# Two block products on half of the tokens ahead of a feed-forward stage, in place of a pair of feature tiles in token halves

## The chip, the cores and the metric

The kernel runs on one core of one Trainium2 chip. The metric is the device time of one execution in microseconds (us), lower is better. Of the kernel before, three runs are known: 2374.69 (median), 2373.43 and 2375.28 us.

## The reference

Two layers on 512 tokens of width 1024. In each layer a feed-forward stage stands before and another behind a mixing stage (three kinds of attention, whose results are gated and merged):

```python
def _swiglu(t, w_gate, w_up, w_down):
    return (jax.nn.silu(t @ w_gate) * (t @ w_up)) @ w_down

f = _swiglu(_rmsnorm(h, ffn1_pre_g[l]), ffn1_w_gate[l], ffn1_w_up[l], ffn1_w_down[l])
h = h + 0.5 * _rmsnorm(f, ffn1_post_g[l])
...                                     # mixing: h = h + rmsnorm(merged @ w_out)
f = _swiglu(_rmsnorm(h, ffn2_pre_g[l]), ffn2_w_gate[l], ffn2_w_up[l], ffn2_w_down[l])
h = h + 0.5 * _rmsnorm(f, ffn2_post_g[l])
```

The hidden width is 2816, that is 22 feature tiles of 128. All is float32. The change concerns the four feed-forward stages alone, called a0, c0 (layer 0) and a1, c1 (layer 1).

## The kernel before

**Numbers in two parts.** TensorE reads a float32 operand here as a high part (rounded to the type fp32r) and a low part (the rest). `split` (L185) makes them: ScalarE casts the high part (L188), VectorE subtracts it from the source to get the low (L189; L191 and L192 where a scale is applied). `mm3` (L212) makes a product of three matmuls: high by high (L214), and two of high by low (L215, L216). A unit of weights is 128 x 1024 numbers, 512 KB. It is fetched by a DMA of the queue SP (`fetch`, at most four in the ring called raw), and split into the rings wh and wl of four units each, or into other places named by `tags`.

**Two ways to multiply.** A *plain pair* is two feature tiles: `gates` (L824) computes the gate of both for all 512 tokens, 48 matmuls of 512 columns, and `ups` (L831) the up part; `hidden` (L659) multiplies Silu(gate) by up. *Block products* compute four feature tiles at once: tokens and model width are halved, gate and up are the two column blocks of the weights, and seven products of 256 tokens by 512 of width by 512 columns, 24 matmuls each, take the place of eight (`gate_up`, L730). Products 0 and 1 need only the activations of the first 256 tokens; 6 needs those of the second 256; 2 to 5 need sums of activation blocks (`sums`, L696: VectorE, with `whole`, L681, `block_sum`, L687, and the splits into the tiles ag). The weight sides of products 2, 3, 5 and 6 are differences as well: VectorE subtracts (L337, L340, L345, L349) before the split. Product 0's sum stays in two PSUM banks through products 3, 5 and 6. After each product the banks are copied by ScalarE (L751) or added by VectorE (L753) into tiles c, and L760 multiplies the two halves of a result. PSUM has eight banks, four called mm and four called z.

**The order of a stage** (`ffn`, L644). Feature tiles 16 and 17 (`EARLY`) are computed by `halved` (L797): half 0, with the tokens of tiles 0 and 1, may run while the token tiles 2 and 3 are still being normalized and transposed (`Sub.chain`, L623); half 1 follows when all are ready. Each half is 96 matmuls of 256 columns, high parts first. Its weights `ug` and `uu` are loaded in the stage before, which is told of them in `marks["early"]`. Then come the gates of pair 18 with Silu at once (`ahead`), the groups of block products for tiles 0 to 15 (`TG`, first group in the order `FIRST`, others in `ORDER`), and between the pieces the calls of `sums`. The down stage (`product`, L871, in the same seven products, on z banks) follows, with the ups of pair 18 and the pair 20 between its products.

**The queue.** `Queue` (L372) holds the jobs of TensorE in this order. When a job starts, its units are loaded, and after that four units of the following jobs (`load_ahead`, L413) unless `hold` is set; `weave` (L455) lets the chain of a token tile come in between at times counted in TensorE's work. The framework under it places semaphores and buffers, and settles the final order in each engine's queue with a model of its own; `in_order` (L166) and `keep_in_program_order` fix parts by hand.

**The kernel's start** (`begin`, L1639). Stage a0 has no stage before it. `begin` fetches the token tiles and first weights, spreads a gain row over the partitions into two mm banks by matmuls (`spread`, L550), computes the statistics, scales (L1676), transposes (L1667) and splits the first two tiles, all in one order for ScalarE and VectorE; the gains are copied to SBUF at L1706 behind the scaling of tile 2.

The early job as it stands:

```python
Q.add(ug + uu, lambda: halved(EARLY, ug, uu, 0), src.ready((0, 1)))
Q.add([], lambda: halved(EARLY, ug, uu, 1), src.ready(range(NT)))
...
add_sums()
Q.add(pairs[0][0], lambda: gates(18, pairs[0][0], True))
add_sums()
todo = turns(TG[0])
some(8)
```

Of the kernel before, what the change touches and what calls it, by code (L numbers as in the profile page):

```python
# [9 lines left out]
F32 = mybir.dt.float32  # L10
F32R = mybir.dt.float32r
BF16 = mybir.dt.bfloat16
AF = mybir.ActivationFunctionType
# [4 lines left out]
P = 128  # L18
# [4 lines left out]
def kernel(  # L23
# [620 lines left out]
    def ffn(l, src, wg, wu, wd, dst, name, spare, aside=None):  # L644
# [152 lines left out]
        def halved(f, ug, uu, half):  # L797
            if half == 0:
                st["p"] = [pbank("mm", f"p{x}{name}_{f + m}") for x in "gu" for m in range(2)]
            else:  # L800
                Q.hold, Q.pinned = False, True
                Q.load_ahead()
                Q.pinned = False
                next(summed)
            c = HALVES[half]

            for uns, pts in ((ug, st["p"][:2]), (uu, st["p"][2:])):
                for low in (False, True):
                    for un in uns:
                        for k, (m, pt) in itertools.product(range(un.nk), enumerate(pts)):  # L810
                            kk, cols = un.k0 + k, slice(m * P, (m + 1) * P)
                            wh, wl = un.h[:, k, cols], un.l[:, k, cols]
                            ah, al = act(kk, c)
                            if low:
                                nc.tensor.matmul(pt[:, c], wh, al, start=False, stop=False, skip_group_check=True)
                                nc.tensor.matmul(pt[:, c], wl, ah, start=False, stop=kk == ND - 1, skip_group_check=True)
                            else:
                                nc.tensor.matmul(pt[:, c], wh, ah, start=kk == 0, stop=False, skip_group_check=True)
                            yield (1 + low) * S // 2 * PE_US
            if half == 1:  # L820
                for m in range(2):
                    hidden(f + m, st["p"][m], st["p"][2 + m])
# [110 lines left out]
        marks["early"] = ug + uu  # L933
        for un, place in zip(ug + uu, ("tri", "tri", (spare, spare), (spare, spare))):
            un.tags = place
# [6 lines left out]
        pairs = [(wpair(wg[l], ND, f * P, f"g{name}_{f}"), wpair(wu[l], ND, f * P, f"u{name}_{f}")) for f in (18, 20)]  # L942
# [8 lines left out]
        for g in TG[1:]:  # L951
            todo = turns(g)
            some(2)
            over, later[:] = later[1:], later[:1]
            behind()
            some(7)
            later[:] = over
        todo = downs(0)
# [680 lines left out]
    def begin():  # L1639
# [9 lines left out]
        ug = Q.jobs[0][0]  # L1649
        for un in ug[2:]:  # L1650
            un.place = "v"
        for un in ug[:2]:
            un.fetch()
        nc.sync.dma_start(hT[2][:], x[0, 2 * P:3 * P, :])
        for un in ug[2:]:
            un.fetch()
# [21 lines left out]
        with in_order(nc.scalar, nc.vector):  # L1678
            r = stats(0)
            for hf in range(2):  # L1680
                scaled(0, hf, r)
            r = stats(1)
            warm(2)
            for hf in range(2):
                turn(0, hf)
            low0 = ug[0].split_from(ug[0].raw[:], later=True)
            for hf in range(2):
                scaled(1, hf, r)
            turn(1, 0)
            turn(1, 1)  # L1690
            low1 = ug[1].split_from(ug[1].raw[:], later=True)
            lows[0, 0]()
            lows[1, 0]()
            low0()
            ug[0].loaded()
            lows[0, 1]()
            lows[1, 1]()
            low1()
            ug[1].loaded()
            r = stats(2)  # L1700
            for hf in range(2):
                scaled(2, hf, r)
            for un in ug[2:]:
                un.load()
            for pt, c in zip(sub.spread, HF):
                nc.scalar.copy(sub.gq[:, c], pt[:])  # L1706
            sub.squared(hT[3][:], sub.sh[3], 0, sub.fs[3][:])
            sub.normed(3)
# [58 lines left out]
```

## Time and profile before

| | |
|---|---|
| runs | 2373.43, 2374.69, 2375.28 us |
| the profiled execution's own time | 2375.59 us |
| its span, first to last instruction | 2373.9 us |
| matmuls | 11688 |
| granted TensorE clock, mean | 0.999 |
| DMA, mean | 147 GB/s |

The page names engines PE (TensorE matmul), PEld (its weight load), DVE (VectorE), ACT (ScalarE), POOL and SP. Matmuls are pipelined and their ends are modelled: a matmul of 512 columns is listed with 0.39 us though the next begins 0.227 us later, so spacing and the length of stretches tell more than the duration of one. In a row of waits stand the waiter, the one waited for, the total in us, the number of waits and the longest. In a row of the timeline stand start, length (us), engine, line, operation, tiles out<-in, shapes, count, and in brackets the idle time before it with what ended it. Tiles of the c stages end in c (wl_tc: low of the block weights of a gate-up product), of the a stages in a.

### The profile page before, as it was taken

To read this page: it belongs to the slowest core of one execution; us is meant where nothing else is said; L and a number is where in the kernel's file an instruction comes from. 1 tells how busy PE (TensorE), PEld (TensorE's weight loads), DVE (VectorE), ACT (ScalarE), POOL (GpSimd) and SP (SyncE) were. 2 spreads that over 40 slices of the span, in tenths; PEclk is the share of its full clock that TensorE was granted. 3 is DMA by queue.
4 is the path that set the end of the run, shared out by engine and by line. 5 is a ranking of instruction groups with operands and counts; after the bars stand their busy time and mean duration, and the time that the engine had idled before them with its cause. 6 is when DMAs were issued, how large, how long until landed. Compare 5 with 4: busy or idle time off the path is not lost.

```text
span 2373.9 us, 31089 instructions
## 1 busy us (share of the span) xinstructions
PE 2362.5 (100%) x11688; PEld 1997.1 (84%) x11688; DVE 1868.3 (79%) x2532; ACT 1412.3 (59%) x2292; POOL 73.9 (3%) x130
## 2 busy tenths in 40 slices
PE   9999999999999999999999999999999999999998
PEld 8888888888888898888888888888888888888887
DVE  8888977778776688889787789766787766877895
ACT  5766555677665555565655665656675655556654
POOL 1000000001110000000000000000001100000000
PEclk9999999999999999999999999999999999999999
DMA  6555565222323445645646455632232244464553
GB/s 213 192 181 169 170 236 144 72 72 80 88 64 118 157 159 165 218 143 165 233 142 210 149 184 195 208 104 80 63 90 80 72 139 145 160 199 157 178 169 133
DMA packets 232603, 349.73 MB, mean 147 GB/s; under 512 B 10730, under 2 KB 117506, under 8 KB 231940
## 3 DMA queue, kind: packets, MB, share of 16 engines
q1 hardware_dynamic: 232352, 347.71, 45.9%
q8 instruction: 92, 1.51, 0.3%
q14 instruction: 59, 0.48, 0.1%
q0 software_dynamic: 96, 0.03, 0.0%
q10 hardware_dynamic: 4, 0.00, 0.0%
HBM read 333.02 MB, written 14.68 MB: 146 GB/s over the span
## 4 chain that ended last, share of the span: by engine, by line
PE 97%; DVE 2%; ACT 1%; DMA 0%; issue 0%; DVEq 0%; SPq 0%; ACTq 0%
PE pta L215 4%; PE pta L214 4%; PE pta L216 4%; PE ptc L214 4%; PE ptc L215 4%; PE ptc L216 4%; PE pg L214 4%; PE pg L216 4%; PE pg L215 4%; PE pdc L216 3%; PE pdc L214 3%; PE pdc L215 3%; PE pda L216 3%; PE pda L215 3%; PE pda L214 3%; PE pb L214 2%
## 5 line engine op out<-in xcount | busy, mean ns | idle before, releaser
L214 PE MATMUL pg<-us_a,wh_wg 128*128 128x512 f32 x384 | 151.0, 393 | 0.0
L216 PE MATMUL pg<-us_a,wl_wg 128*128 128x512 f32 x384 | 149.7, 390 | 0.0
L215 PE MATMUL pg<-us_a,wh_wg 128*128 128x512 f32 x384 | 149.6, 390 | 0.0
L188 ACT CAST wh_tc<-ktc 128x1024 fp32r<-128x1024 f32 x80 | 84.3, 1054 | 64.3 <-PE ptc L216 34.5
L188 ACT CAST wh_ta<-kta 128x1024 fp32r<-128x1024 f32 x80 | 84.2, 1053 | 55.6 <-PE pta L216 30.4
L189 DVE TENSOR_TENSOR wl_tc<-ktc,wh_tc 128x1024 fp32r<-128x1024 f32 x80 | 97.7, 1222 | 23.4 <-ACT wh_tc L188 23.2
L189 DVE TENSOR_TENSOR wl_ta<-kta,wh_ta 128x1024 fp32r<-128x1024 f32 x80 | 97.6, 1221 | 21.7 <-ACT wh_ta L188 21.5
L214 PE MATMUL pta<-wh_ta,aga 128*128 128x512 f32 x256 | 100.3, 392 | 0.1
L214 PE MATMUL ptc<-wh_tc,agc 128*128 128x512 f32 x256 | 100.3, 392 | 0.0
L215 PE MATMUL pta<-wl_ta,aga 128*128 128x512 f32 x256 | 99.7, 390 | 0.4 <-DVE wl_ta L189 0.4
L215 PE MATMUL ptc<-wl_tc,agc 128*128 128x512 f32 x256 | 99.7, 389 | 0.0
L216 PE MATMUL ptc<-wh_tc,agc 128*128 128x512 f32 x256 | 99.3, 389 | 0.0
L216 PE MATMUL pta<-wh_ta,aga 128*128 128x512 f32 x256 | 99.3, 389 | 0.0
L216 PE MATMUL pda<-wh_da,ala 128*128 128x512 f32 x224 | 87.4, 390 | 0.2 <-DVE ala L189 0.2
L216 PE MATMUL pdc<-wh_dc,alc 128*128 128x512 f32 x224 | 87.4, 390 | 0.0
L214 PE MATMUL pdc<-wh_dc,ahc 128*128 128x512 f32 x224 | 87.4, 390 | 0.0
L214 PE MATMUL pda<-wh_da,aha 128*128 128x512 f32 x224 | 87.3, 390 | 0.0
L215 PE MATMUL pda<-wl_da,aha 128*128 128x512 f32 x224 | 87.2, 389 | 0.0
L215 PE MATMUL pdc<-wl_dc,ahc 128*128 128x512 f32 x224 | 87.2, 389 | 0.0
L216 PEld LDWEIGHTS pg<-us_a,wl_wg 128*128 128x128 f32 x384 | 72.1, 188 | 15.3
L215 PEld LDWEIGHTS pg<-us_a,wh_wg 128*128 128x128 f32 x384 | 72.2, 188 | 14.1
L214 PEld LDWEIGHTS pg<-us_a,wh_wg 128*128 128x128 f32 x384 | 72.1, 188 | 14.1
(543 smaller groups left out, 7515.6 us busy)
## 6 DMA issues: line engine op xcount, KB each, us to landing
raw_ta<-in_ffn_w_gate_dram SPq DMA_DIRECT2D x64, 512.0 KB, 3.9
raw_tc<-in_ffn_w_gate_dram SPq DMA_DIRECT2D x64, 512.0 KB, 3.9
raw_da<-in_ffn_w_down_dram SPq DMA_DIRECT2D x58, 512.0 KB, 3.8
raw_dc<-in_ffn_w_down_dram SPq DMA_DIRECT2D x58, 512.0 KB, 3.7
raw_wg<-in_w_gate_dram SPq DMA_DIRECT2D x48, 512.0 KB, 3.7
kta<-in_ffn_w_up_dram SPq DMA_DIRECT2D x32, 512.0 KB, 6.1
ktc<-in_ffn_w_up_dram SPq DMA_DIRECT2D x32, 512.0 KB, 5.6
raw_wo<-in_w_out_dram SPq DMA_DIRECT2D x24, 512.0 KB, 3.4
```

The source lines that it names most:

```text
L188: both = [nc.scalar.copy(h_ap, src)]
L189: make = lambda: nc.vector.tensor_tensor(l_ap, src, h_ap.bitcast(F32), ALU.subtract)
L214: nc.tensor.matmul(pt, lh, rh, start=start, stop=False, skip_group_check=free)
L215: nc.tensor.matmul(pt, lh, rl, start=False, stop=False, skip_group_check=free)
L216: nc.tensor.matmul(pt, ll, rh, start=False, stop=stop, skip_group_check=free)
```

## The change

`halved` goes. In its place stand products 0 and 1 of the first group, in a function `direct` that runs each product's parts high by high, low by high, high by low. In the three stages that follow another sub-layer, product 0's result is copied into the two banks of product 1, so that Silu can read product 1's banks at once; in a0 the two are added by VectorE as before. Once all tokens are ready, `opening` runs the early pair's gates as a plain pair, and its ups follow after the second call of `sums`. The gates of pair 18 move into the down stage, three products ahead of its ups, and their Silu is computed with `hidden`. The weights fetched by the stage before are those of products 0 and 1. In `begin` the order of ScalarE's and VectorE's work changes: both units of product 0 are cast early, the scalings of tiles 0 and 1 and their transposes are interleaved, and product 1's weights are split ahead of the statistics of tile 2 (before: the up weights behind its scaling).

```diff
-                yield uns, (lambda n=n, uns=uns: gate_up(f, n, uns, top))
+                if f == TG[0] and n < 2:
+                    yield uns, (lambda n=n, uns=uns: direct(f, n, uns))
+                else:
+                    yield uns, (lambda n=n, uns=uns: gate_up(f, n, uns, top))
...
-        def halved(f, ug, uu, half):
...
+        def direct(f, n, uns):
+
+            seeded = n == 1 and src.name != "x"
+            if n == 0:
+                st["gb", 0] = [pbank("mm", f"pt{name}_{f}_0_{e}") for e in range(2)]
+                if src.name != "x":
+                    st["gb", 1] = [pbank("mm", f"pt{name}_{f}_1_{e}") for e in range(2)]
+                else:
+                    st["c", 0, 0] = stile([P, 2, S], "f", f"c{name}_{f}_00", F32)
+            elif not seeded:
+                st["gb", 1] = [pbank("mm", f"pt{name}_{f}_1_{e}") for e in range(2)]
             else:
...
+                st["c", 0, 0] = stile([P, 2, S], "f", f"c{name}_{f}_00", F32)
+            pts = st["gb", n]
+            parts = ((0, 0), (1, 0), (0, 1))
+            for ia, iw in parts:
+                for e, un in itertools.product(range(2), uns):
+                    for k in range(un.nk):
+                        kk = un.k0 + k
+                        first = ia == iw == 0 and kk == 0 and not seeded
+                        last = n == 1 and iw == 1 and kk == ND // 2 - 1
+                        nc.tensor.matmul(pts[e][:], input_block(n, kk, e)[ia], (un.h, un.l)[iw][:, k], start=first,
+                                         stop=last, skip_group_check=True)
+                        yield S * PE_US
+                    if iw and un is uns[-1]:
+                        if n == 0 and src.name != "x":
+                            nc.scalar.copy(st["gb", 1][e][:], pts[e][:])
+                        elif n == 0:
+                            nc.scalar.copy(st["c", 0, 0][:, e], pts[e][:])
+                        else:
+                            t = st["c", 0, 0][:, e]
+                            if not seeded:
+                                nc.vector.tensor_tensor(t, t, pts[e][:], ALU.add)
+                            nc.scalar.activation(t, pts[e][:] if seeded else t, AF.Silu)
...
-        Q.add(ug + uu, lambda: halved(EARLY, ug, uu, 0), src.ready((0, 1)))
-        Q.add([], lambda: halved(EARLY, ug, uu, 1), src.ready(range(NT)))
+
+        def opening():
+            Q.hold, Q.pinned = False, True
+            Q.load_ahead()
+            Q.pinned = False
+            next(summed)
+            yield from gates(EARLY, ug, True)
+
+        todo = turns(TG[0])
+        (n0, run0), (n1, run1) = itertools.islice(todo, 2)
+        marks["early"] = n0 + n1
+        for un, place in zip(n0 + n1, ("tri", "tri", (spare, spare), (spare, spare))):
+            un.tags = place
+        Q.add(n0, run0, src.ready((0, 1)))
+        Q.add(n1 + ug, run1)
+        Q.add([], opening, src.ready(range(NT)))
...
-        Q.add(pairs[0][0], lambda: gates(18, pairs[0][0], True))
+        Q.add(uu, lambda: ups(EARLY, uu))
         add_sums()
-        todo = turns(TG[0])
-        some(8)
+        some(6)
...
-        some(1)
+        Q.add(pairs[0][0], lambda: gates(18, pairs[0][0]))
+        some(3)
         Q.add(pairs[0][1], lambda: ups(18, pairs[0][1]))
-        some(7)
+        some(2)
...
         with in_order(nc.scalar, nc.vector):
-            r = stats(0)
-            for hf in range(2):
-                scaled(0, hf, r)
-            r = stats(1)
+            r0 = stats(0)
+            scaled(0, 0, r0)
+            r1 = stats(1)
+            scaled(0, 1, r0)
             warm(2)
-            for hf in range(2):
-                turn(0, hf)
-            low0 = ug[0].split_from(ug[0].raw[:], later=True)
-            for hf in range(2):
-                scaled(1, hf, r)
+            lw = [n0[0].split_from(n0[0].raw[:], later=True)]
+            turn(0, 0)
+            scaled(1, 0, r1)
+            scaled(1, 1, r1)
+            lw.append(n0[1].split_from(n0[1].raw[:], later=True))
             turn(1, 0)
-            turn(1, 1)
-            low1 = ug[1].split_from(ug[1].raw[:], later=True)
             lows[0, 0]()
             lows[1, 0]()
-            low0()
-            ug[0].loaded()
+            for un, low in zip(n0, lw):
+                low()
+                un.loaded()
+            turn(0, 1)
+            turn(1, 1)
             lows[0, 1]()
             lows[1, 1]()
-            low1()
-            ug[1].loaded()
+            for un in n1:
+                un.load()
             r = stats(2)
             for hf in range(2):
                 scaled(2, hf, r)
-            for un in ug[2:]:
-                un.load()
```

More of the change, by code (lines that the diff above doesn't have):

```diff
@@ L795, in park @@
                     nc.sync.dma_start(hsave[t], hT[t][:])
-        def halved(f, ug, uu, half):
-            if half == 0:
-                st["p"] = [pbank("mm", f"p{x}{name}_{f + m}") for x in "gu" for m in range(2)]
-            else:
[L801 to L822, printed above, removed]
@@ L957, in ffn @@
             later[:] = over
+        pairs = [(wpair(wg[l], ND, f * P, f"g{name}_{f}"), wpair(wu[l], ND, f * P, f"u{name}_{f}")) for f in (18, 20)]
         todo = downs(0)
@@ L1647, in begin @@
         nc.sync.dma_start(hT[1][:], x[0, P:2 * P, :])
-        ug = Q.jobs[0][0]
-        for un in ug[2:]:
-            un.place = "v"
-        for un in ug[:2]:
+        n0, n1 = Q.jobs[0][0], Q.jobs[1][0][:2]
+        for un in n0:
             un.fetch()
         nc.sync.dma_start(hT[2][:], x[0, 2 * P:3 * P, :])
-        for un in ug[2:]:
+        for un in n1:
             un.fetch()
@@ L1702, in begin @@
                 scaled(2, hf, r)
-            for un in ug[2:]:
-                un.load()
             for pt, c in zip(sub.spread, HF):
```

7 lines of the change are left out of this document (3 added, 4 removed).

## The prediction

> **What bounds the kernel now.** The page comes first: its busy line, its row of granted clocks and its chain.
>
> ```profile
> span 2373.9 us, 31089 instructions
> PE 2362.5 (100%) x11688; PEld 1997.1 (84%) x11688; DVE 1868.3 (79%) x2532; ACT 1412.3 (59%) x2292; POOL 73.9 (3%) x130
> PEclk9999999999999999999999999999999999999999
> PE 97%; DVE 2%; ACT 1%; DMA 0%; issue 0%; DVEq 0%; SPq 0%; ACTq 0%
> ```
>
> TensorE is busy in 2362.5 of 2373.9 us at a full clock, so time can be won in two ways only: fewer TensorE cycles for the same products, or fewer of the last waits. The view of TensorE's waits shows how few those are.
>
> ```profile
> PE ptc L215 <- DVE wl_tc L189: 0.5, 1, 0.5
> PE pta L215 <- DVE wl_ta L189: 0.4, 1, 0.4
> PE pda L216 <- DVE ala L189: 0.2, 1, 0.2
> ```
>
> All three are waits for VectorE. They show where there is no reserve: the low halves of weights in the front of a feed-forward stage, and a factor in the down stage. I therefore read that front by windows, in the second of the four stages (c, first layer). The columns are the stretch, its length, and busy us with instructions of PE, PEld, DVE, ACT, POOL, then clock, DMA share and GB/s.
>
> ```profile
> 866.60:878.15 11.55, 11.55 (x98) 11.55 (x97) 11.55 (x12) 7.56 (x9) 0.00 (x0) 1.00 0.58 175
> 878.15:889.06 10.91, 10.91 (x50) 9.02 (x49) 10.70 (x12) 5.58 (x7) 0.00 (x0) 1.00 0.59 208
> 889.06:899.94 10.88, 10.88 (x49) 9.01 (x48) 10.35 (x10) 5.92 (x8) 0.00 (x0) 1.00 0.60 187
> 866.60:921.88 55.28, 55.28 (x290) 47.52 (x289) 52.87 (x51) 30.59 (x36) 0.00 (x0) 1.00 0.64 209
> 921.88:932.89 11.01, 11.01 (x50) 8.93 (x48) 8.37 (x9) 5.79 (x7) 0.00 (x0) 1.00 0.33 97
> 2097.39:2109.43 12.04, 11.48 (x49) 8.93 (x48) 9.27 (x10) 5.78 (x7) 0.00 (x0) 1.00 0.32 88
> ```
>
> The first three are half 1 of the early pair (96 matmuls of 256 columns; one or two neighbours reach over each edge), the gates of pair 18 (48 of 512) and block products 0 and 1 (24 of 512 each). From half 1 to the next group's first product VectorE is busy in 52.87 of 55.28 us. The front is thus bound by two engines at once. The last row is that first product and its neighbour in the fourth stage: 12.04 us against 11.01 in the row above, because VectorE came late, 1.0 us in all.
>
> **The change, part by part.** *Width.* Half 1 streams as many columns as the 48 gate matmuls, in 11.55 us against 10.91: 0.64 us are lost with each half. There are two halves in each of four stages, and the change turns all of them into matmuls of 512 columns, the number of products being the same: 8 x 0.64 = **-5.1 us**. The Trainium skill ("TensorE: Matmul & The Clock Gate", section "Back-to-back issue gap") gives an isolated spacing of N/2.4 + 2.5 ns; by it a 512-column matmul would save only 2.5 ns against two of 256, an estimate of 384 x 2.5 = 1.0 us in all, and the sum would be 4.1 us worse. The rows say 120 ns (11.55/96) and 227 ns (10.91/48), so the trace does not agree with that small a difference.
>
> *Start of the kernel.* Products 0 and 1 need the first two token tiles, as half 0 does, but product 1 needs two more banks of the four called mm. Two are held by the product, two by the spread gains, until ScalarE has copied these.
>
> ```profile
> 9.17 1.40 DVE L1676 SCALAR_TENSOR_TENSOR fx<-hx,nhx,gqx 128x512 f32<-128x512 f32 x2
> 14.28 1.28 DVE L192 SCALAR_TENSOR_TENSOR us_x<-utx,us_x 128x512 fp32r<-128x512 f32 x2
> 17.32 1.41 DVE L1676 SCALAR_TENSOR_TENSOR fx<-hx,nhx,gqx 128x512 f32<-128x512 f32 x2
> 18.64 2.35 DVE L189 TENSOR_TENSOR wl_ua<-raw_ua,wh_ua 128x1024 fp32r<-128x1024 f32 x2
> 18.10 1.25 ACT L1706 COPY gqx<-gqx 128x512 f32<-128x512 f32 x2 [0.68 <-DVE fx L1676]
> 25.02 1.04 PE L618 MATMUL utx<-ident,fx 128*128 128x128 f32 x8
> 26.37 0.56 PE L818 MATMUL pga<-us_x,w_ga 128*128 128x256 f32 x3
> ```
>
> The copies wait for the scaling of tile 2, which today stands ahead of the second two weight lows (18.64) and in the new order behind them. VectorE's new queue: one more scaling (0.7) puts the first tiles' scalings' end at 11.3 (today 10.6); four activation lows at 0.6, four weight lows at 1.15 and about 0.5 of waiting give 18.8 (product 0's own last low is over near 15.2, so it ends near 17); 0.6 of statistics and the scalings 1.4 give 20.8, and the first bank is free at 20.8. Then 5.44 us for product 1 (half of 10.88) and two sets of eight transposes at 0.9: TensorE opens the early gates at 28.0, where half 1 starts at 26.37 today. That is 1.7 later instead of the 0.64 earlier that the width promises: **+2.3 us**. Bounds: 0 if the banks come in time, 3.3 if tile 3 is a microsecond late as well.
>
> *The first gate matmuls.* Half 1 today runs high parts first. The gates take high, low, high.
>
> ```profile
> 865.88 1.09 ACT L191 ACTIVATE us_b<-utb 128x512 fp32r<-128x512 f32 x2 [2.65 <-PE utb L618]
> 866.51 0.69 DVE L192 SCALAR_TENSOR_TENSOR us_b<-utb,us_b 128x512 fp32r<-128x512 f32 x1 [2.45 <-ACT us_b L191]
> 866.60 2.12 PE L818 MATMUL pgc<-us_b,w_gc 128*128 128x256 f32 x16
> 870.76 1.28 ACT L656 ACT_TABLE_LOAD   x1
> 872.35 1.09 ACT L656 ACTIVATE sc<-pgc 128x512 f32<-128x512 f32 x2 [0.31 <-PE pgc L816]
> 880.21 1.28 DVE L661 TENSOR_TENSOR sc<-puc,sc 128x512 f32<-128x512 f32 x2
> ```
>
> Those sixteen high matmuls cover the low of tile 3, ready at 867.2. The second gate matmul would stand at 866.83: 0.4 us of waiting in each of the three stages that follow another sub-layer, **+1.2** (0 to 2). The Silu of product 1 moves ahead of the gates, and the bank it frees is the gates' own. Its table load (1.28) waits for nothing, as at 870.76, where it is over before the Silu's input comes; ScalarE's 2.65 us of idling hide it at nothing. If the two casts of the early gates' weights, which now go there too, take that cover, load and Silu cost up to 1.9 us in three stages, 5.7 in all. The seed copies after product 0 fall into the same idle time: nothing, at most one Silu's length (0.5) in each of three stages.
>
> *Two banks less.* Product 0's sum keeps two mm banks, so product 2 now needs the bank of the up matmuls just before it. TensorE reaches it three matmuls (0.68) after they end; the multiply that frees it lasts 0.68 behind a matmul's tail of 0.16. Lower bound 0.2 us; upper bound 2.6, as today's pair of multiplies is over at 881.5, 3.3 us after the products' end at 878.15. I take 0.3, near the lower end, because what delays them today is work for which nothing waits yet: four stages, **+1.2**.
>
> *VectorE's time.* The gates of pair 18 (10.9 us of TensorE) leave this front, and products 0 and 1 stand ahead of it.
>
> ```profile
> 911.20 1.23 DVE L337 TENSOR_TENSOR ktc<-ktc,raw_tc 128x1024 f32<-128x1024 f32 x1 [0.24 <-DMA raw_tc<-in_ffn_w_gate_dram]
> 914.12 1.22 DVE L337 TENSOR_TENSOR ktc<-ktc,raw_tc 128x1024 f32<-128x1024 f32 x1 [0.56 <-DMA raw_tc<-in_ffn_w_gate_dram]
> 915.27 1.22 DVE L189 TENSOR_TENSOR wl_tc<-ktc,wh_tc 128x1024 fp32r<-128x1024 f32 x1
> 917.78 1.22 DVE L189 TENSOR_TENSOR wl_tc<-ktc,wh_tc 128x1024 fp32r<-128x1024 f32 x1
> 920.45 1.23 DVE L189 TENSOR_TENSOR wl_tc<-raw_tc,wh_tc 128x1024 fp32r<-128x1024 f32 x1 [0.31 <-ACT wh_tc L188]
> 921.88 0.39 PE L214 MATMUL ptc<-wh_tc,us_b 128*128 128x512 f32 x1
> ```
>
> Today the low that the next group needs is ready at 921.68, its matmul stands at 921.88: no lead. In the new order TensorE has eight half-windows of 5.44, 43.5 us, between the opening of the gates and that product. VectorE loses four weight lows (4 x 1.14) and two adds (1.2), 5.8 of its 52.87, and swaps two lows of pair 18 for the ups': 47.1. In today's order that is 3.6 us too much. But the window holds work for later: product 6's two subtractions and two lows (915.27, 917.78), 4.5, and the two subtractions at 911.20 and 914.12, 2.3; without them 40.3, and 3.2 to spare. So VectorE's lateness costs between nothing and 3.6 a stage. The nearest row is the wait of 0.5 for wl_tc above: I take 0.5 in the two stages that today show no such wait, **+1.0**, and leave today's as they are (they might go too, -1.4 in all: 1.0 by the windows and the 0.4 for wl_ta).
>
> *Pair 18 in the down stage.*
>
> ```profile
> 1058.04:1118.00 59.96, 59.96 (x273) 49.69 (x272) 54.59 (x67) 35.49 (x49) 0.00 (x0) 1.00 0.49 158
> ```
>
> There VectorE has 54.59 of 59.96 us; 10.9 us of gates with two lows (2.3) and two Silus on ScalarE relieve it, so the move costs nothing and the wait for ala goes, **-0.2**. The two 512 KB loads go with the gates; at 209 GB/s in the front and 158 here they are hidden at either place, as are n0's and n1's, the same size as the ones they replace. If that cover fails it is one wait like the fourth stage's, 1.0.
>
> *Sum:* -5.1 + 2.3 + 1.2 + 1.2 + 1.0 - 0.2 = +0.4. The profiled execution took 2375.59 us (span 2373.9 and 1.7 around it), so 2376.0 for its like. The median of the runs shown, 2374.69, is 0.9 below it: the forecast is **2375.1 us**, the gain eaten by new waits.
>
> **Rivals.** *Faster: the waits are all covered.* TensorE's own cycles are certain; each wait above rests on an order of VectorE's and ScalarE's queues that may be better. Then -5.1 of width, -0.2 in the down stage and -1.4 of today's waits, 6.7 off the median: **2368.0**. For it: VectorE has 3.2 us to spare by need. Against: at 921.68 it has no lead at all, and the start's bank is held by a chain that I can count.
>
> *Slower: VectorE sets the pace of the front.* It keeps today's order and each front lacks the 3.6 us: 4 x 3.6 = 14.4 in place of my 1.0 and of today's 1.4, that is +12.0 on the forecast: **2387.1**. It decides from the point at which VectorE's work ahead of the next group's first product is over 43.5 us; the place is product 5 to that product. For it: the shortening is 11.8 us and only 5.8 of work goes. Against: the work ahead of need.
>
> *The width saves nothing*, because the weight load and not the columns makes the spacing in the new places: the 5.1 stays away, **2380.2**. Against: 227 ns stand in the windows of gates and block products alike. The Trainium skill's formula above, which leaves 1.0 of the 5.1, would come out near this rival.
>
> **Numbers.** A difference of under 0.2% (4.7 us) is about what a measurement of this kernel can't tell from none. Forecast, from 2370.0 to 2379.4: 0.48. Faster rival: 0.28. VectorE: 0.20. Width: 0.04. So faster 0.28, same 0.48, slower 0.24. The range goes from all waits covered to VectorE at its full price, 2366.5 to 2387.1; beyond lie further waits at the bounds named (Silu, banks).
>
> **What would show it.** Right: no matmul of 256 columns in these four places, 227 ns in theirs; a gap of some 3.8 us on TensorE between 17 and 20.8 us ahead of product 1, ended by the gain copies; short waits at the first gate for us_b and at product 2 for sc; VectorE busy over 95% from the gates to the next group. Wrong: the gates of the first stage opening before 26.4 us; waits of several us for wl_t at products 5, 6 or the next group's first; a wait of the gates for Silu; new waits in the down stage.

## The result

The changed kernel takes 2384.9 us (median of five runs, 2383.71 to 2386.91), the kernel before 2374.69 (five runs). The ratio is 1.0044, with a 95% interval of 1.003 to 1.0059: the change costs about 10 us. The profiled execution took 2386.91 us, its span is 2385.2 against 2373.9. The median lies inside the range on record and 9.8 us above the forecast, on the side to which it gave a chance of 0.24.

The page of the changed kernel, its span, busy line and chain:

```profile
span 2385.2 us, 30322 instructions
PE 2364.0 (99%) x11304; PEld 1979.6 (83%) x11304; DVE 1863.4 (78%) x2526; ACT 1410.1 (59%) x2295; POOL 73.1 (3%) x130
PE 94%; DVE 3%; ACT 1%; DMA 1%; issue 1%; POOL 0%; DVEq 0%; ACTq 0%; SPq 0%; POOLq 0%
```

There are 384 matmuls fewer, as the change says. TensorE should be busy for 5 us less, yet it is listed with 1.5 us more: matmuls at the low clock that is shown below count as busy for longer. VectorE's share of the chain grows from 2% to 3%. The view of TensorE's waits says where TensorE stands still (its rows for these four stages):

```profile
PE utx L618 <- DVE fx L1698: 5.3, 1, 5.3
PE utb L618 <- DVE nhb L508: 4.6, 2, 2.8
PE utc L618 <- DVE nhc L508: 0.5, 1, 0.5
PE pgc L215 <- DVE us_b L192: 0.5, 2, 0.2
PE pga L215 <- DVE us_x L192: 0.2, 1, 0.2
PE pga L215 <- DVE us_c L192: 0.2, 1, 0.2
PE pta L214 <- DVE sa L661: 0.2, 1, 0.2
```

L618 is the transposes of a token tile. In all four stages TensorE now waits to transpose token tile 2, because that tile isn't normalized yet. The waits for the block weights, wl_tc and wl_ta, which the kernel before has, are gone from this view; what is left of them is shown at the end of the next section.

Where the time went can be counted. Taking every start-to-start distance of two matmuls over the usual one of their shape (227 ns for 512 columns, 120 for 256, 109 for 128), and adding these up by stage, gives the time that TensorE lost in waiting or at a low clock. A stage is counted here from its first matmul to that of the next stage, so a0 and a1 have the mixing stage behind them in it. "Less 1.28" takes off what two halves of 0.64 us save. Every length is that of one profiled execution; that of the changed kernel was the slowest of its five runs, 2.0 us above their median.

| stage | length before | after | difference | more time lost | less 1.28 of width |
|---|---|---|---|---|---|
| a0 | 840.8 | 847.4 | +6.6 | 8.2 | 6.9 |
| c0 | 338.8 | 340.3 | +1.5 | 2.7 | 1.4 |
| a1 | 836.6 | 837.1 | +0.5 | 1.7 | 0.4 |
| c1 | 345.1 | 348.3 | +3.2 | 4.5 | 3.2 |

The width's saving, two halves of 0.64 us in each stage, is there everywhere, and the new losses are larger. The losses of a0 and c1, the two largest, are not all waiting. By windows (the columns are those of the prediction's windows: the last three are clock, DMA share and GB/s), a0's wait and what follows it, and the stretch behind c1's wait:

```profile
17.50:23.20 5.70, 0.35 (x3) 0.04 (x1) 4.32 (x8) 2.21 (x5) 0.00 (x0) 0.93 0.88 285
23.20:33.40 10.20, 10.20 (x40) 8.17 (x41) 6.44 (x11) 5.21 (x12) 0.00 (x0) 0.70 0.81 274
2045.20:2053.90 8.70, 8.64 (x40) 7.12 (x40) 4.01 (x6) 4.19 (x9) 0.00 (x0) 0.80 0.61 210
```

After the idling the granted clock is 0.70 and 0.80 for some microseconds. Here is the same place of a0 in the timeline of TensorE:

```profile
23.19 0.66 PE L618 MATMUL utx<-ident,fx 128*128 128x128 f32 x2 [5.35 <-DVE fx L1698]
23.71 3.35 PE L821 MATMUL pta<-wh_ta,us_x 128*128 128x512 f32 x7
33.42 0.45 PE L214 MATMUL pga<-us_x,wh_ga 128*128 128x512 f32 x1
```

Seven matmuls of product 1 take 3.35 us, where seven at 227 ns take about 1.8. The gates open at 33.42; the prediction said 28.0. So a0 pays 5.5 us of idling, some 3.0 of low clock, and 0.6 at the first gates, together 9.1; the old opening had small losses of its own, hence 8.2 in the table.

### The profile page after: what moved, and what is told of

It reads as the page before. It is cut to its first block, busy times and chain, and to the rows that moved or that the text cites. A ratio compares the mean times of both kernels' runs of the same rounds, so it can differ in the third digit from the quotient of the medians.

```text
span 2385.2 us, 30322 instructions
## 1 busy us (share of the span) xinstructions
PE 2364.0 (99%) x11304; PEld 1979.6 (83%) x11304; DVE 1863.4 (78%) x2526; ACT 1410.1 (59%) x2295; POOL 73.1 (3%) x130
## 4 chain that ended last, share of the span: by engine, by line
PE 94%; DVE 3%; ACT 1%; DMA 1%; issue 1%; POOL 0%; DVEq 0%; ACTq 0%; SPq 0%; POOLq 0%
PE ptc L215 4%; PE ptc L214 4%; PE ptc L216 4%; PE pta L214 4%; PE pta L216 4%; PE pta L215 4%; PE pg L216 4%; PE pg L214 4%; PE pg L215 4%; PE pda L216 3%; PE pda L215 3%; PE pda L214 3%; PE pdc L216 3%; PE pdc L214 3%; PE pdc L215 3%; PE pb L215 2%
```

## Why tile 2 is late

VectorE's timeline in a0, ahead of the scaling of tile 2 that TensorE waits for (L1698 in this kernel's lines):

```profile
18.02 0.15 DVE L508 TENSOR_SCALAR nhx<-nhx 128x1 f32<-128x1 f32 x1
18.28 1.23 DVE L189 TENSOR_TENSOR wl_ga<-raw_ga,wh_ga 128x1024 fp32r<-128x1024 f32 x1
20.71 1.23 DVE L189 TENSOR_TENSOR wl_ga<-raw_ga,wh_ga 128x1024 fp32r<-128x1024 f32 x1 [1.21 <-ACT wh_ga L188]
22.29 1.41 DVE L1698 SCALAR_TENSOR_TENSOR fx<-hx,nhx,gqx 128x512 f32<-128x512 f32 x2
```

Between the statistics of tile 2 (18.02) and its scaling (22.29) stand the lows of the weights of the early pair's gates (wl_ga). The change loads these with product 1 (`Q.add(n1 + ug, run1)`), and nothing pins them, so they came to stand inside the chain of tile 2, and the second even waited there 1.21 us for its cast. In c1 the same happens, and more:

```profile
2035.57 1.22 DVE L189 TENSOR_TENSOR wl_gc<-raw_gc,wh_gc 128x1024 fp32r<-128x1024 f32 x1
2040.78 1.23 DVE L337 TENSOR_TENSOR ktc<-ktc,raw_tc 128x1024 f32<-128x1024 f32 x1 [2.06 <-DMA raw_tc<-in_ffn_w_gate_dram]
2041.92 0.21 DVE L514 SCALAR_TENSOR_TENSOR nfb<-nfb 128x1 f32<-128x1 f32 x1
2045.10 1.22 DVE L337 TENSOR_TENSOR ktc<-ktc,raw_tc 128x1024 f32<-128x1024 f32 x1
```

L337 is the weight subtraction for product 2, some 35 us ahead of its use. It stands between the small steps of tile 3's and tile 2's normalization, and at 2040.78 it holds VectorE for 2.06 us until its DMA lands and for 1.23 more. In c0 it stands at 862.02, for 0.75 and 1.23 us, and TensorE's idling there is 2.0 us. How long it waits for its DMA isn't the same in every execution, as e6_warm shows below.

There is a second side to it. TensorE waits so long only because the transposes of tile 2 stand at once behind product 0, after 24 matmuls (in a1, where the wait is short, after 37); in c0 of the kernel before they stand after 68 of half 0's 96. My theory had therefore two parts, with a rival each:

- *Late on VectorE*: the unpinned weight work (gate lows, L337) makes the tile late. Rival: it is the new order of the start and the seed copies on ScalarE.
- *Early on TensorE*: with the transposes further back in its queue the same lateness would cost nothing. Rival: they must wait wherever they stand.

And of the prediction's own rival, VectorE as the pace of the front, the changed kernel shows little. The lows of product 2's weights are over by 888.2, and its first matmuls stand at 896.75 and 896.97 (timelines of VectorE and TensorE, c0):

```profile
887.01 1.22 DVE L189 TENSOR_TENSOR wl_tc<-ktc,wh_tc 128x1024 fp32r<-128x1024 f32 x1
```

```profile
896.75 0.39 PE L214 MATMUL ptc<-wh_tc,agc 128*128 128x512 f32 x1
896.97 0.39 PE L215 MATMUL ptc<-wl_tc,agc 128*128 128x512 f32 x1
```

That is 8.7 us of lead at the first low. Whether this margin belongs to the change or to one part of it is tested below too. At product 6, four products later, nothing is left of it:

```profile
917.43 1.22 DVE L189 TENSOR_TENSOR wl_tc<-raw_tc,wh_tc 128x1024 fp32r<-128x1024 f32 x1
918.70 0.19 PEld L215 LDWEIGHTS ptc<-wl_tc,us_b 128*128 128x128 f32 x1 [0.23 <-DVE wl_tc L189]
918.73 0.47 PE L215 MATMUL ptc<-wl_tc,us_b 128*128 128x512 f32 x1
919.03 0.40 PE L216 MATMUL ptc<-wh_tc,us_b 128*128 128x512 f32 x1
```

The weight load of product 6's second matmul waits for a low that VectorE ends at 918.65, and the matmul behind stands 0.30 us later and not 0.23. So the front has no reserve there, but the price is small: about 0.1 us in c0 and in a1, and 0.3 in c1, where the kernel before lost 1.1.

## The experiments

Ratios are to runs of the kernel before taken beside each group: 2375.53 us for the first four, 2375.44 for the next four, 2376.62 for the last three (medians). The lengths of the stages are read as in the table above, in us. They come from one execution each, so where they and the ratio disagree on a size, the ratio is the surer one.

| kernel | time | ratio, 95% interval | a0 | c0 | a1 | c1 |
|---|---|---|---|---|---|---|
| before | 2374.69 | | 840.8 | 338.8 | 836.6 | 345.1 |
| changed | 2384.90 | 1.0044 (1.003 to 1.0059) | 847.4 | 340.3 | 837.1 | 348.3 |
| e1_ug_later | 2384.17 | 1.0033 (1.002 to 1.0046) | 844.2 | 340.9 | 836.3 | 347.5 |
| e2_pin | 2382.18 | 1.0028 (1.0019 to 1.0038) | 847.8 | 339.3 | 836.9 | 344.4 |
| e3_both | 2378.39 | 1.0011 (1.0002 to 1.002) | 843.8 | 339.2 | 836.5 | 344.3 |
| e4_noseed | 2382.14 | 1.0026 (1.0016 to 1.0035) | 846.7 | 338.9 | 837.1 | 344.1 |
| e5_pair_alone | 2413.08 | 1.0158 (1.0144 to 1.0172) | 852.1 | 348.1 | 846.2 | 353.4 |
| e6_warm | 2390.35 | 1.0061 (1.0047 to 1.0074) | 852.7 | 340.9 | 836.9 | 345.8 |
| e7_mixed | 2386.31 | 1.0045 (1.0033 to 1.0058) | 851.7 | 339.7 | 836.6 | 344.4 |
| e8_mixed_noseed | 2386.39 | 1.0043 (1.0031 to 1.0056) | 851.7 | 339.1 | 837.3 | 344.0 |
| e9_a0_whole | 2376.16 | 0.9998 (0.9989 to 1.0006) | 840.7 | 340.8 | 836.5 | 344.6 |
| e10_products_alone | 2386.15 | 1.0041 (1.0028 to 1.0055) | 848.3 | 340.4 | 836.9 | 344.7 |
| e11_reorder | 2379.08 | 1.001 (1.0002 to 1.0019) | 842.7 | 339.5 | 836.6 | 345.1 |

### e1_ug_later: the early gates' weights behind tile 3

```diff
-        Q.add(n1 + ug, run1)
-        Q.add([], opening, src.ready(range(NT)))
+        Q.add(n1, run1)
+        Q.add(ug, opening, src.ready(range(NT)))
+        def between():
+            Q.pinned = True
+            for un in ug:
+                un.load()
+            Q.pinned = False
+        src.between = between
```

`between` is called by the token chain right behind `normed(3)`, the issue of tile 3's normalization, in `begin` as well.

> The changed kernel with one thing moved: the early gates' weights are split behind the normalization of token tile 3, pinned there, not with the start of product 1. Theory A (VectorE's and ScalarE's queues: these two splits, 2 x 1.2 us of lows and 2 x 1.05 of casts, stand inside the normalization of tile 2, and TensorE, which has tile 2's transposes next, stands idle for it): the wait for the scaling in the first stage falls from 5.3 to some 2 us and most of the half-clock stretch behind it goes, the waits in the other three fall by about 2 us each: 2384.9 down to 2373 to 2378. Theory B (the seed copies of product 1 behind tile 3's Square are what TensorE waits for): the first stage gains as above, the others nothing: 2379 to 2381. Theory C (product 2's subtractions, one of which waits for its DMA in VectorE's queue): the first stage gains, the others stay: as B, but with a wait of VectorE for raw still standing ahead of the transposes.

a0 gets 3.2 us shorter (844.2), c0 0.6 longer and c1 0.8 shorter (340.9, 347.5); the time, 2384.17, lies above what any of the three theories gave. In c0 and c1 the transposes of tile 2 come in time now, but a new wait stands at the first gates; the rows are from TensorE's waits and from VectorE's timeline in c0:

```profile
PE pgc L215 <- DVE us_b L192: 2.4, 2, 1.2
```

```profile
870.88 1.23 DVE L337 TENSOR_TENSOR ktc<-ktc,raw_tc 128x1024 f32<-128x1024 f32 x1 [1.72 <-DMA raw_tc<-in_ffn_w_gate_dram]
872.03 1.28 DVE L192 SCALAR_TENSOR_TENSOR us_b<-utb,us_b 128x512 fp32r<-128x512 f32 x2
```

The subtraction L337 has only moved on: it now stands ahead of tile 3's low and waits 1.72 us there for its DMA, with the low behind it. Moving the gate lows alone helps a0 in part, and not c0 or c1.

### e2_pin: product 2's subtraction held in the written order

```diff
-                nc.vector.tensor_tensor(t, t, self.raw[:], ALU.subtract)
+                ins = nc.vector.tensor_tensor(t, t, self.raw[:], ALU.subtract)
+                if Q.pinned:
+                    tc.keep_in_program_order(ins)
```

> The changed kernel with product 2's two weight subtractions pinned behind what is traced ahead of them, so that they can't come in front of the token tiles' normalization. Theory A (the early gates' splits are the delay): under 1 us a stage in c0, a1, c1: 2382 to 2385. Theory C (the subtractions are): the 1.04 and 0.86 us for which VectorE waits and the 1.2 to 2.4 us that they last go from the path: c0 gains 2 us, c1 3 us with the half clock, a1 0.5: 2378 to 2380. Theory B (seeds): no change.

c1 gets 3.9 us shorter and c0 1.0; the two waits of together 4.6 us for tile 2 are down to 0.7:

```profile
PE utb L620 <- DVE fb L610: 0.7, 2, 0.4
```

a0 is as late as ever. So c0 and c1 lost their time to L337. The time itself, 2382.18, lies in the range of theory A (2382 to 2385) and above that of theory C, whose mechanism the waits show: C had reckoned with 5.5 us, the stages give back 4.9, and the ratios, 1.0028 against 1.0044, some 4.

### e3_both

The two edits together.

> Both edits: early gates' weights behind the normalization of tile 3, and product 2's subtractions pinned. Theory A with C: no wait of TensorE over 1 us is left in the opening of c0, a1 and c1, some 2 us in a0: 2369 to 2374. Theory B (seeds): waits of 1 to 2 us stay at product 1 in c0 and c1, ended by the copies: 2376 to 2379.

The ratio falls from 1.0044 to 1.0011: about three quarters of the loss come back. As theory A with C said, no wait of over 1 us is left in the openings of c0, a1 and c1; but the time, 2378.39, misses its range (2369 to 2374) and lies in that of the rival, whose waits for the seed copies are half a microsecond each and not 1 to 2. What is left stands mostly in a0, in TensorE's waits:

```profile
PE utx L620 <- DVE fx L1710: 1.8, 1, 1.8
PE pga L214 <- DVE ca L836: 1.7, 1, 1.7
PE ptc L825 <- ACT ptc L830: 0.9, 2, 0.5
```

Tile 2 is still 1.8 us late in a0. The gates then wait 1.7 for a bank that is free only when VectorE has added product 1 (L836), and that add stands behind the gate lows in their new place. The seed copies (last row) cost 0.5 in c0 and in c1.

### e4_noseed: the changed kernel without the seed copies

Product 0 is copied to SBUF by ScalarE and added to product 1 by VectorE in all four stages, as a0 does it. Nothing is pinned.

```diff
-            seeded = n == 1 and src.name != "x"
+            seeded = False
```

> The changed kernel without seeds: in all four stages product 0 is copied to SBUF and product 1's banks are added to it by VectorE, as in a0. Theory B (TensorE waits for the seed copies, and tile 2's transposes were put ahead of product 1 because of them): transposes of tile 2 move back into product 1, the waits of c0 and c1 go: 2377 to 2379. Theory A (the chain of the token tiles is late on VectorE): the waits stay or move by under 0.5 us, VectorE has 1.2 us more a stage: 2384 to 2388.

c0 and c1 come back as in e2_pin, by 1.4 and 4.2 us, and the time, 2382.14, is that of e2_pin too, between the ranges of the two theories. This happens though the gate lows and L337 still stand inside the token chain. The difference is on TensorE's side (timeline, c0):

```profile
864.33 2.65 PE L816 MATMUL ptc<-wh_tc,us_b 128*128 128x512 f32 x11
866.83 1.06 PE L618 MATMUL utb<-ident,fb 128*128 128x128 f32 x8
```

Eleven matmuls of product 1 now stand ahead of the transposes of tile 2, which start at 866.83, as late as in the changed kernel (866.86), and nobody waits. Without a seed product 1 needs nothing from ScalarE and begins at once; with the seed the framework put the transposes first, presumably because its model has product 1 wait for the copies. Both parts of the theory hold: the tile is late, and it is asked for early, and either cure is enough in c0 and c1. The rival that the transposes must wait wherever they stand falls. a0 is seedless already, and keeps its wait of 4.4 us here.

### e5_pair_alone: the kernel before with pair 18's gates in the down stage

```diff
-        Q.add(pairs[0][0], lambda: gates(18, pairs[0][0], True))
         add_sums()
         todo = turns(TG[0])
...
+        Q.add(pairs[0][0], lambda: gates(18, pairs[0][0]))
+        some(3)
         Q.add(pairs[0][1], lambda: ups(18, pairs[0][1]))
```

> The kernel before with one part of the change alone: the gates of pair 18 stand in the down stage, their Silu with the multiply. Theory (VectorE has room in the front, so moving 10.9 us of TensorE work out of it costs nothing; the stage accounting of after says within 0.1 a stage): within 1 us of the kernel before, and no wait for wl_t of over 1 us at products 5, 6 or the next group's first. Rival (VectorE sets the pace of the front as soon as 10.9 us of TensorE work with only 2.3 us of VectorE work leave it): up to 3.6 us in each of four stages, 14.4 us in all, with waits for wl_t.

The kernel gets 38 us slower, far more than either expectation. Every stage shows one long wait at product 2; in c0 (TensorE's waits, VectorE's timeline, TensorE's timeline):

```profile
PE pta L214 <- ACT wh_ta L188: 14.3, 2, 8.3
PE ptc L214 <- ACT wh_tc L188: 12.0, 2, 6.0
```

```profile
894.02 1.22 DVE L189 TENSOR_TENSOR agc<-rc,agc 128x1024 fp32r<-128x1024 f32 x1
895.16 1.22 DVE L687 TENSOR_TENSOR rc<-rc,rc 128x1024 f32<-128x1024 f32 x1
896.30 2.36 DVE L337 TENSOR_TENSOR ktc<-ktc,raw_tc 128x1024 f32<-128x1024 f32 x2
898.57 2.35 DVE L189 TENSOR_TENSOR agc<-rc,agc 128x1024 fp32r<-128x1024 f32 x2
900.84 2.35 DVE L189 TENSOR_TENSOR wl_tc<-ktc,wh_tc 128x1024 fp32r<-128x1024 f32 x2
```

```profile
899.12 0.39 PE L216 MATMUL ptc<-wh_tc,us_b 128*128 128x512 f32 x1
905.51 1.39 PE L214 MATMUL ptc<-wh_tc,agc 128*128 128x512 f32 x2 [6.01 <-ACT wh_tc L188]
```

VectorE works without a pause, sums of activations first, and comes to product 2's subtractions only at 896.30; TensorE is done with product 1 at 899.4 and stands still for 6.2 us, after which six matmuls go at half clock. This is the prediction's slower rival in the flesh, at another place (product 2) and 8 to 11 us a stage where it said 3.6. It decides in this order of products and not in that of the changed kernel. The edit does one thing more: it brings the two calls of `sums` together, ahead of product 0. Whether the missing 10.9 us of TensorE's work or this order of VectorE's work does the harm was not told apart.

### e10_products_alone: the changed kernel with pair 18's gates in the front

```diff
         Q.add(uu, lambda: ups(EARLY, uu))
+        Q.add(pairs[0][0], lambda: gates(18, pairs[0][0], True))
         add_sums()
```

> The changed kernel with the gates of pair 18 left in the front, behind the early pair's ups: the other part of the change alone. Theory (with products 0 and 1 ahead VectorE has had their four lows behind it, and product 2 waited only 0.2 us in the changed kernel, so pair 18's 10.9 us are no cover that is missed): within 1 us of the changed kernel, 2385. The two parts then don't add: 38 us for the one alone, 10 for the other alone, 10 for both. Rival (the waits of the changed kernel come from pair 18's absence, as in e5_pair_alone): 5 us or more faster than the changed kernel.

2386.15 us, not to be told from the changed kernel. The parts of the change don't add: the pair alone costs 38 us, the products alone 10, both 10. Products 0 and 1 take the place in which pair 18's gates served as cover: their four lows are done before the token chain ends, and the lead of 8.7 us at product 2 comes with that, as I read it; no run took the lows alone away. In this kernel L337 doesn't come to stand in the token chain, and the waits for tile 2 in c0 and c1 are short without any pin, which bears e2_pin out:

```profile
PE utb L618 <- DVE fb L608: 0.6, 2, 0.3
```

c1 is 3.6 us shorter by it in this execution, while a0 is 0.9 longer and c0 loses 1.1 us in its down stage. Why the medians don't show the difference stays open, and so equal times don't prove that pair 18's gates are free at either place to better than 2 or 3 us.

### e6_warm: an attempt to keep the clock up

22 matmuls on zeros, their result unused, ahead of the transposes of tile 2 in a0.

```diff
             yield ("wait", us_)
+            if t == 2:
+                wp2 = pbank("z", "warm2")
+                for _ in range(22):
+                    tc.keep_in_program_order(nc.tensor.matmul(wp2[:], wsb[:, 0:P], wsb[:, 0:S], start=True, stop=True))
             sub.turned(t)
```

> The changed kernel with 22 matmuls on zeros (bf16, 512 columns, into a spare bank, their result unused) in TensorE's queue between product 0 and the transposes of tile 2 in a0, where TensorE idles for 5.5 us. Theory (the idling itself lowers the granted clock, and the low clock costs as much again as the wait): a0 gets 3.1 us shorter, the matmuls behind 23 us stand at 227 ns, in all 3 us faster than the changed kernel (about 2382). Rival (the clock is low there for another reason, or the slower matmuls are covered by the chain of tile 3): no more than 0.5 us.

The experiment doesn't answer its question. The framework put seven matmuls of product 1 ahead of the 22, so these ran in TensorE's own time at 26.75 us and not in the gap; a0 is 5.3 us longer. It shows another thing, the wait that the prediction had counted on at this place:

```profile
PE pta L821 <- ACT gqx L1727: 4.3, 1, 4.3
```

With product 1 in front, it waits for the two banks of the spread gains until 23.6 us. The prediction's mechanism exists, some 3 us later than it said (20.8), and in the changed kernel it is hidden behind the transposes' wait for the same scaling. And c1, whose program the edit doesn't touch, is 2.5 us shorter than in the changed kernel's profile:

```profile
2045.10 1.22 DVE L337 TENSOR_TENSOR ktc<-ktc,raw_tc 128x1024 f32<-128x1024 f32 x1 [0.50 <-DMA raw_tc<-in_ffn_w_gate_dram]
```

The subtraction waits 0.50 us for its DMA here and not 2.06; TensorE stands for 1.4 us and not 2.9, and no low clock follows. So the 3 to 4 us of c1 hold for that execution, not for every one.

### e7_mixed and e8_mixed_noseed: a0 opened as before

e3_both with the early pair in halves and the old start in a0, and the new opening in c0, a1 and c1; e8 without seed copies besides. Pair 18's gates stand in all four down stages.

```diff
-                if f == TG[0] and n < 2:
+                if f == TG[0] and n < 2 and name != "a0":
...
+        if name == "a0":
+            Q.add(ug + uu, lambda: halved(EARLY, ug, uu, 0), src.ready((0, 1)))
+            Q.add([], lambda: halved(EARLY, ug, uu, 1), src.ready(range(NT)))
```

> The two edits of e3_both, but stage a0 opens as in the kernel before (half 0 and half 1 of the early pair, the old order of the start); the new opening stands in c0, a1 and c1, the gates of pair 18 in all four down stages. Theory (what e3_both still lost to the kernel before lay in a0, 3.05 us): 2375.3, a0 at 840.8 within 0.3, c0 339.2, a1 836.5, c1 344.3. Rival (the loss of a0 comes back in later stages): 2378.4. If the width were worth its 1.28 us in each of three stages with nothing lost, it would be 2371.

> As e7_mixed, and product 0's sum is copied to SBUF by ScalarE and added to product 1 by VectorE, in place of the seed copies into product 1's banks. Theory (with the chain on time the seed copies still cost about 0.9 us in c0 and c1, as the waits of e3_both say): 1 to 2 us faster than e7_mixed. Rival (the add takes the place of the copies: the gates wait for the bank behind the add, as in e4_noseed at 871.28, 0.8 to 1.0 us): within 0.5 us of e7_mixed.

c0, a1 and c1 of e7_mixed are as expected, a0 is 10.9 us too long, by one wait and the low clock behind it (TensorE's waits of e7_mixed):

```profile
PE pta L214 <- ACT wh_ta L188: 8.3, 1, 8.3
```

It is e5_pair_alone's wait: I had put the old opening together with the moved pair, on the strength of a reading that said the pair was free. e8 gives the same time as e7: c0 and c1 gain 0.6 and 0.4, a1 loses 0.7, and waits for us_b and ca take the seed copies' place, as the rival said.

### e9_a0_whole: a0 wholly as before

As e7_mixed, with pair 18's gates in a0's front again.

> As e7_mixed, but a0 is whole as in the kernel before: the gates of pair 18 too stand in its front again. c0, a1 and c1 keep the new opening with the two edits of e3_both, and pair 18's gates in their down stages. Theory (e7_mixed lost its 11 us in a0 alone, where product 2 waited 8.3 us for its weights because pair 18's gates no longer stood ahead of it, as in e5_pair_alone, and c0, a1 and c1 together gain what they lose): a0 840.8, c0 339.4, a1 836.6, c1 344.3, in all 2375.3, the same as the kernel before within 2 us. Rival (the loss of e7_mixed lies elsewhere): 2386.

a0 is 840.7, and the time, 2376.16 at a ratio of 0.9998 (0.9989 to 1.0006), is that of the kernel before. Only c0 differs from the expectation, by 1.4, most of it a wait for a factor in its down stage:

```profile
PE pdc L216 <- DVE alc L189: 1.0, 1, 1.0
```

The new opening, cured in three stages, gains 1.28 us of width in each and gives about as much back, at the first gates, at the seed copies, and in c0 in the down stage.

### e11_reorder: tile 2 ahead of product 1's weights

e3_both, with the splits of n1 behind the scaling of tile 2 and the copies of the gains in `begin`.

```diff
-            for un in n1:
-                un.load()
             r = stats(2)
             for hf in range(2):
                 scaled(2, hf, r)
             for pt, c in zip(sub.spread, HF):
                 nc.scalar.copy(sub.gq[:, c], pt[:])
+            for un in n1:
+                un.load()
```

> e3_both, and at the start of a0 the statistics and scaling of tile 2 and the copies of the gains stand ahead of the splits of product 1's weights, not behind them. Theory (what is left of a0's loss is tile 2 late by the two splits of product 1's weights): the wait of tile 2's transposes goes from 2.0 us to under 0.8, a0 from 843.9 to 842.7, in all 1.2 us faster than e3_both (2377.2). Rival (what is late next takes its place: product 1 waits for its own weights): no faster than e3_both, 2378.4, with a wait for wl_ta or wh_ta of a microsecond or more.

a0 comes to 842.7 as the theory said, the wait of tile 2's transposes to 0.3 or less, and in its place stands the rival's (TensorE's waits):

```profile
PE pta L825 <- ACT wh_ta L188: 1.9, 2, 1.7
PE pga L214 <- DVE ca L836: 1.3, 1, 1.3
```

Product 1 waits 1.7 us for its own weights. The whole kernel is no faster than e3_both (1.001 against 1.0011): the 1.1 us of a0 are missing again in c0 and c1 of the profiled execution, whose program the edit doesn't touch. None of these runs gets the products, the gate weights and tile 2 into a0's first 30 us without some wait of 1 to 2 us for VectorE or ScalarE; the best a0 with the new opening is still 1.9 us over the old one.

## The prediction, point by point

- **Width, -5.1: right.** Product 0's 24 matmuls take 5.42 us in c0 and the early pair's 48 ups 10.90, which is 227 ns each, and each stage's length agrees with 1.28 saved. This speaks against the rival that the width saves nothing.

```profile
859.48:864.90 5.42, 5.42 (x25) 4.29 (x23) 4.33 (x9) 2.40 (x8) 0.00 (x0) 1.00 0.90 317
885.85:896.75 10.90, 10.90 (x50) 9.01 (x49) 10.87 (x12) 5.76 (x7) 0.00 (x0) 1.00 0.01 2
```

- **Start of the kernel, +2.3: the step that failed most.** The stage lost 6.6. The gap of "some 3.8 us between 17 and 20.8 us" came as 5.5, from 17.7 to 23.2; the scaling of tile 2 ended it and not the gain copies, as the transposes came ahead of product 1. "VectorE's new queue" lacked the lows of the early gates' weights, which the diff puts with product 1: they took its time from 18.28 to 21.85 ahead of the scaling. e1_ug_later gives back 3.2 us of it, e3_both leaves 1.8 of the wait. I had counted the instructions of the rewritten block in `begin` and not those of the job that it starts. The half clock behind the gap, about 3.0 us, was in no term.
- **First gates, +1.2: the mechanism right, the size too small (2.9).** In c0, a1 and c1 each, 0.27 us pass ahead of the first gate and 0.50 between it and the second (which waits for us_b as said), 2.3 in all, and 0.6 in a0.
- **Table load, Silu and seed copies, nothing: half wrong.** No matmul waits for the Silu. But the prediction gave the reason by which it could fail, "if the two casts of the early gates' weights, which now go there too, take that cover", at up to 1.9 us a stage. Such work did take cover away, not Silu's but the token chain's: 2.0 us in c0, 2.9 and 1.4 of low clock in c1 (1.4 and none in e6_warm's execution), 0.6 in a1. The weight subtractions of product 2, the larger part by e2_pin, were in my sum of VectorE's time and not in its order.
- **Two banks less, +1.2: too dear.** One wait of 0.2 for sa at product 2, in a0.
- **VectorE's pace, +1.0: too dear, and misread.** As its sign said, VectorE is busy for over 95% from the gates to product 6 (42.55 of 44.15 us in c0). It has 8.7 us of lead at product 2 and none at product 6, at 0.1 to 0.3 us a stage, and c1 loses 0.8 less there than before. The matmul at 921.88 in the kernel before, which the prediction calls the next group's first, is product 6 of the first group: behind it ScalarE applies Silu straight to the product's banks (L749), which the kernel does for product 6 and never for a product 0.

```profile
927.42 0.60 ACT L749 ACTIVATE cc<-ptc 128x512 f32<-128x512 f32 x1 [0.98 <-PE ptc L216]
```

So product 6's subtractions and lows were no work for later, and neither the 3.2 us to spare nor the 3.6 us lacking, both worked out for this place, came about.

- **Pair 18, -0.2: not contradicted for this change** (e10_products_alone, which can't tell so small a difference), and for a reason that the prediction didn't give. It argued from what relieves the down stage and asked of the front only whether VectorE's pace would bind. In the old order the same move costs 38 us at once (e5_pair_alone).
- **The slower rival, VectorE sets the pace of the front at 14.4 us: not what happened.** The time came out near its 2387.1 for another cause, the token chain, which e2_pin, e3_both and e4_noseed show. That the measured time lies inside the range is luck: the range's upper end was this rival's price, and the terms of the sum held only a part of what took the time. (Its lower end, 2366.5, stands without a sum; the fastest case worked out was 2368.0.)

## What to carry to other kernels

When a change moves a job's loads, list what every loaded unit issues on each engine, and ask of each whether anything pins its place: unpinned work 35 us ahead of its use can stand in front of a short chain that TensorE needs now, and hold it for a DMA besides. The place of the waiter matters as much as that of the late work (with the seed copies the transposes stood 11 matmuls further forward, at 1 to 4 us in c0 and c1). The parts of a change need not add: price each alone and together before calling one free. And read a stage's size from more than one execution where a DMA stands in the chain.

## What the hardware showed besides

The granted clock falls to half after short idling, and the line is sharp in these thirteen profiles, counted from a0's first matmul. After each of the twelve stretches in which TensorE stood for 2.9 us or more (2.9, 4.0, 4.5 to 4.9, 5.5, 6.2, 8.5), 6 to 11 of the next matmuls of 512 columns stood 427 ns apart and not 227; after none of the sixteen of 1.0 to 2.0 us did any. The low clock lasts some 3 to 6 us and costs 1.4 to 3.1. In c1 of the changed kernel it set in only 1.3 us after TensorE had resumed. The Trainium skill ("TensorE: Matmul & The Clock Gate", "Part 1: The HAM clock gate") puts it at one idle window of about 3.4 us, free-running, with a spacing of N/1.2 ns while cold. The 427 ns agree; in these runs 2.9 us were enough. That idling is the cause is argued from these 28 places; the one run that was to fill a gap with work, e6_warm, missed it, so it was not shown by itself.
